# A start-up history load moved from GpSimd's casting queue to SyncE as fp32, with casting loads issued ahead of the identity

## Chip, cores, metric

One core of one Trainium2 chip. The metric is device time in microseconds (us) of that core for one execution.

## The reference

A causal convolution along the sequence with matrix taps: eight shifted copies of `x`, each multiplied by a 512x512 matrix, summed in fp32.

```python
B, S, D, K = 8, 4096, 512, 8          # x: (B, S, D), kernel: (K, D, D), fp32
for k in range(K):
    shifted = x moved k steps down the sequence, zeros in front
    out += np.matmul(shifted, kernel[k])
```

## The kernel before

The sequence is cut into 256-step runs, one run on each of the 128 partitions. The kernel works in bf16 and replaces the eight taps by a three-level scheme of sums and differences: three "nodes" (LO, HI, MID) a step, each of a few 512-wide products. Sums of `x` go to tiles `D4`, `D42`, `D41`, `D421`, `T4`...; differences of weights (`mid_dve`) go to `W[...MID...]`. Only the head of the program is touched by the change. It needs a **history**: the last 7 steps of the run before, which lies one partition lower, so 127 rows are loaded into partitions 1 to 127 (partition 0 and every 16th have no run before them and get zeros).

```python
def load(out, src):                               # casting fp32 -> bf16 load, GpSimd's queue
    nc.gpsimd.dma_start(out=out, in_=src)
...
H = D421                                          # bf16
load(H[1:P, 4:8], xr[0:P - 1, RUN - 4:RUN, :])    # history: 127 rows of 8 KB
load_x(0, 0)
ident = spool.tile([P, P], bf, name="ident")
make_identity(nc, ident)
identh = ...                                      # ident with every 16th column zeroed (GpSimd)
identn = ...                                      # -ident (GpSimd); not used in the head
...
def sums_pe(name, k, *sums):                      # transposes AND adds x and history on TensorE:
    ...                                           # matmul(x, ident) + matmul(H, identh) in one bank
for r in range(2):
    for k in range(4):
        fill(pair(k))                             # 16 dummy matmuls through ident
...
load_w(4)
transpose_pe("xh", 2, H, 5, 8)
sums_pe("d4a", 1, (-4, 0), (-3, 1))
load(H[1:P, 1:4], xr[0:P - 1, RUN - 7:RUN - 4, :])   # second history load, 6 KB rows
load_w(6)
sums_pe("d4b", 2, (-2, 2), (-1, 3))
...                                               # load_w(5), load_w(7)
direct(0, 2)                                      # first products: 16 "direct" ones of 4 matmuls
...
node_a1(1)                                        # first product of the first node
```

`xin` tiles have two buffers, refilled by `load_x` on GpSimd's queue.

```python
mpool = ctx.enter_context(tc.tile_pool(name="m", bufs=2))
...
    elif n.a == MID:
        ms[b_] = mpool.tile([P, 2, D], f32, name="ms")
        nc.scalar.copy(out=ms[b_], in_=p)         # waits for the buffer's earlier store
```

## Time and profile before

| | before |
|---|---|
| time, median of 3 runs | 783.0 us (782.42 to 783.3) |
| span of the profiled run | 780.9 us |
| TensorE | 767.4 us busy, 98% |
| VectorE / ScalarE | 84% / 36% |
| last product ends | 776.35 us |

What a change of the head can win or lose is the time up to 776.35 us in which no product runs: some 24 us in this kernel, 21.2 of them before 28.99 us.

### The profile page before, as it was taken

What the parts mean: (1) busy time and instruction counts of PE and PEld (TensorE: products, weight loads), DVE (VectorE), ACT (ScalarE), POOL (GpSimd) and SP (SyncE); (2) the same over time, 40 slices, a digit from 0 to 9 for tenths busy, and PEclk for the clock granted to TensorE, in tenths of its full rate; (3) what the DMA queues carried; (4) which work ended last, traced back from release to release, by engine and by line L of the source; (5) the groups of instructions that cost most, each with busy time, mean ns of one, the idle gap of its engine ahead of it and who ended that gap; (6) DMA issues with size and microseconds to landing.
All of it is one profiled execution on the core that took longest, in us unless ns stands there. A gap on an engine that the chain in (4) does not pass through costs nothing.

```text
span 780.9 us, 9507 instructions
## 1 busy us (share of the span) xinstructions
PE 767.4 (98%) x3620; PEld 349.0 (45%) x3620; DVE 659.3 (84%) x764; ACT 283.2 (36%) x460; POOL 42.8 (5%) x83
## 2 busy tenths in 40 slices
PE   7899999999999999999999999999999999999997
PEld 4444444444444444444444444444444444444443
DVE  4899888888888889888898888898888898888895
ACT  2453433333333333343324343333343333343332
POOL 5000000000000000000000000000000000000000
PEclk9999999999999999999999999999999999999999
DMA  9963979778788777878777788877787877788753
GB/s 163 210 120 114 237 176 207 169 187 167 178 179 206 174 176 173 177 184 194 184 171 168 179 190 188 191 166 179 165 187 187 195 170 182 166 172 200 179 153 123
DMA packets 159229, 138.37 MB, mean 177 GB/s; under 512 B 130130, under 2 KB 134226, under 8 KB 159184
## 3 DMA queue, kind: packets, MB, share of 16 engines
q1 hardware_dynamic: 145312, 98.84, 46.3%
q0 software_dynamic: 13728, 38.66, 31.1%
q8 instruction: 28, 0.46, 0.2%
q10 hardware_dynamic: 144, 0.26, 0.1%
q14 instruction: 17, 0.14, 0.1%
HBM read 77.32 MB, written 67.11 MB: 185 GB/s over the span
## 4 chain that ended last, share of the span: by engine, by line
PE 94%; DMA 3%; DVE 1%; POOL 1%; issue 0%; ACT 0%; DVEq 0%; POOLq 0%
PE pp L215 94%; DMA xin<-in_x_dram 2%; DMA XT<-xin 1%; POOL w L80 0%; DVE D L76 0%; PE pp L192 0%; DVE pp L76 0%; ACT XT L390 0%; DVE y L76 0%; POOL D L80 0%; DVEq L648 0%; POOL xin L80 0%; POOL identn L148 0%; PE pp L186 0%; POOL ident masks.py:199 0%
## 5 line engine op out<-in xcount | busy, mean ns | idle before, releaser
L215 PE MATMUL pp<-w,D 128*128 128x512 bf16 x3280 | 715.8, 379 | 1.7 <-DMA w<-in_kernel_dram 0.9
L215 PEld LDWEIGHTS <-D 128*128 128x128 bf16 x3280 | 320.2, 98 | 390.4 <-issue 2.8
L76 DVE TENSOR_TENSOR D<-D 128x2048 bf16<-128x2048 bf16 (+2 forms) x250 | 227.2, 948 | 3.4 <-ACT D L369 3.4
L76 DVE TENSOR_TENSOR y<-pp,ms 128x1024 f32<-128x1024 f32 (+1 forms) x121 | 146.4, 1212 | 45.3 <-PE pp L215 45.3
L76 DVE TENSOR_TENSOR D<-XT 128x2048 bf16<-128x2048 bf16 (+2 forms) x153 | 142.5, 947 | 12.1 <-DMA XT<-xin 10.4
L262 ACT COPY pp<-pp 128x512 f32<-128x512 f32 x95 | 54.1, 570 | 260.6 <-PE pp L215 260.6
L274 ACT COPY pp<-pp 128x512 f32<-128x512 f32 x95 | 54.2, 570 | 167.1 <-PE pp L215 165.6
L76 DVE TENSOR_TENSOR pp<-dts,pp 128x512 f32<-128x512 f32 x95 | 65.7, 691 | 43.9 <-ACT dts L280 42.6
L317 ACT COPY ms<-pp 128x1024 f32<-128x1024 f32 x60 | 61.0, 1016 | 35.0 <-PE pp L215 33.0
L80 POOL DMA_DIRECT2D xin<-in_x_dram x64 | 34.0, 531 | 692.5 <-DMA XT<-xin 675.8
L290 DVE SCALAR_TENSOR_TENSOR pp<-pp,dts 128x512 f32<-128x512 f32 x95 | 66.0, 695 | 3.2
L280 ACT COPY dts<-pp 128x512 f32<-128x512 f32 x95 | 57.5, 606 | 0.0
L276 ACT ACTIVATE pp<-pp 128x512 f32<-128x512 f32 x95 | 56.1, 590 | 0.8 <-PE pp L215 0.8
L215 PE MATMUL pp<-w,XT 128*128 128x512 bf16 x120 | 30.8, 379 | 0.0
L76 DVE TENSOR_TENSOR w<-w,w 128x2048 bf16<-128x2048 bf16 x19 | 22.9, 1219 | 1.5 <-DMA w<-in_kernel_dram 1.3
L215 PEld LDWEIGHTS <-XT 128*128 128x128 bf16 x120 | 11.7, 98 | 14.2
L186 PE MATMUL pp<-zero,ident 128*128 128x512 bf16 x20 | 6.7, 493 | 3.1 <-POOL ident masks.py:199 3.1
L215 PE MATMUL pp<-w,F 128*128 128x512 bf16 x36 | 8.7, 379 | 0.2 <-DVE pp L76 0.2
L215 PE MATMUL pp<-w,w 128*128 128x512 bf16 x36 | 8.3, 379 | 0.0
L192 PE MATMUL pp<-ident,xin 128*128 128x128 bf16 x48 | 3.2, 219 | 3.6 <-DMA xin<-in_x_dram 1.4
L80 POOL DMA_DIRECT2D w<-in_kernel_dram x8 | 6.1, 785 | 0.5 <-DMA w<-in_kernel_dram 0.5
L358 DVE COPY D<-pp 128x1536 bf16<-128x1536 bf16 x1 | 1.0, 958 | 6.1 <-PE pp L192 6.1
(59 smaller groups left out, 78.7 us busy)
## 6 DMA issues: line engine op xcount, KB each, us to landing
out_dram<-y SPq DMA_DIRECT2D x123, 512.0 KB, 3.4
xin<-in_x_dram POOLq DMA_DIRECT2D x64, 512.0 KB, 6.0
w<-in_kernel_dram POOLq DMA_DIRECT2D x8, 512.0 KB, 15.7
out_dram<-ms SPq DMA_DIRECT2D x2, 512.0 KB, 5.4
out_dram<-f SPq DMA_DIRECT2D x2, 512.0 KB, 6.3
XT<-xin SPq DMA_TRANSPOSE x61, 6.1
D<-in_x_dram POOLq DMA_DIRECT2D x1, 508.0 KB, 5.6
D<-in_x_dram POOLq DMA_DIRECT2D x1, 381.0 KB, 9.4
```

The lines of the kernel that those rows point to most:

```text
L76: nc.vector.tensor_tensor(out=o, in0=a, in1=b, op=op)
L80: nc.gpsimd.dma_start(out=out, in_=src)
L186: nc.tensor.matmul(pw[:, h], lhsT=ident, rhs=zero, start=True, stop=True)
L192: nc.tensor.transpose(o[:, t - t0, c * P:(c + 1) * P], src[:, t, c * P:(c + 1) * P], ident)
L215: nc.tensor.matmul(bank, lhsT=comp[:, c * P:(c + 1) * P], rhs=w[:, c, :], start=start and c == 0, stop=c == DC - 1, skip_group_check=True)
L262: nc.scalar.copy(out=n.q[:, 0], in_=n.q[:, 1])
L274: nc.scalar.copy(out=n.p[b_][:, 1], in_=n.q[:, 1])
L276: nc.scalar.mul(out=n.p[b_][:, 1], in_=n.q[:, 1], mul=-1.0)
L280: nc.scalar.copy(out=n.dts, in_=n.q[:, 0])
L290: nc.vector.scalar_tensor_tensor(out=p[:, 0], in0=p[:, 1], scalar=-1.0, in1=n.dts, op0=MUL, op1=SUB)
L317: nc.scalar.copy(out=ms[b_], in_=p)
L358: nc.vector.tensor_copy(out=XF[:, 0:3], in_=bank["xh"])
```

## The change

Its intent, as the edit shows it: take the history off GpSimd's queue, so that `x`, weights and the second history load start sooner; load it as plain fp32 from SyncE and cast it on ScalarE and VectorE; issue the first weight and the second history load before building the identity; replace the small matmuls by transposes and VectorE additions; let the dummy matmuls multiply a tile of zeros, so that they needn't wait for the identity; and build one weight difference with ScalarE and an accumulating DMA instead of VectorE.

```diff
-    H = D421
-    load(H[1:P, 4:8], xr[0:P - 1, RUN - 4:RUN, :])
+    H, HF = XT, D421.bitcast(f32).rearrange("p (t b) d -> p t (b d)", b=2)
+    nc.sync.dma_start(out=HF[1:P], in_=xr[0:P - 1, RUN - 4:RUN, :])
     load_x(0, 0)
-    ident = spool.tile([P, P], bf, name="ident")
-    make_identity(nc, ident)
-    identh = ... ; identn = ...
...
+    def mid_neg(u, v):
+        nc.scalar.mul(out=W[MID, u, v], in_=W[LO, u, v], mul=-1.0)
+    def mid_acc(u, v):
+        nc.gpsimd.dma_start(out=W[MID, u, v], in_=W[HI, u, v], accum_op=ADD)
+
+    load_w(4)
+    load(H[1:P, 1:4], xr[0:P - 1, RUN - 7:RUN - 4, :])
+    ident = spool.tile([P, P], bf, name="ident")
+    make_identity(nc, ident)
...
-    for r in range(2):
-        for k in range(4):
-            fill(pair(k))
+    for k in range(6):
+        fill(pair(k % 4))
...
-    sums_pe("d4a", 1, (-4, 0), (-3, 1))
...
+    transpose_pe("x0", 2, xin[0, 0], 0, 2)
+    nc.scalar.copy(out=H[:, 6:8], in_=HF[:, 2:4])
+    nc.vector.tensor_copy(out=H[:, 4:6], in_=HF[:, 0:2])
+    transpose_pe("h0", 0, H, 4, 6)
+    nc.vector.tensor_copy(out=XF[:, 4:6], in_=bank["x0"])
+    nc.vector.tensor_copy(out=XF[:, 0:2], in_=bank["h0"])
+    first_run(XF[:, 0:2])                         # zeroes every 16th column
...
+    tt(D4[:, 0:2], XF[:, 0:2], XF[:, 4:6], ADD)
+    direct(0, 0)                                  # the first product
...
-    mid_dve(0, HI, LO)
+    mid_neg(HI, LO)                               # and mid_acc(HI, LO) later
```

(Cut: the rest of the head, up to the first regular step, is the same calls in another order, with the loads, stores and transposes of blocks 2 and 3 among them; from that step on the programs agree.)

More of the change, by code (lines that the diff above doesn't have):

```diff
@@ L136, in pair @@
         return ppool.tile([P, 2, D], f32, name=f"pp{k}")
-    H = D421
-    load(H[1:P, 4:8], xr[0:P - 1, RUN - 4:RUN, :])
+    H, HF = XT, D421.bitcast(f32).rearrange("p (t b) d -> p t (b d)", b=2)
+    nc.sync.dma_start(out=HF[1:P], in_=xr[0:P - 1, RUN - 4:RUN, :])
     load_x(0, 0)
-    ident = spool.tile([P, P], bf, name="ident")
-    make_identity(nc, ident)
-    identh = spool.tile([P, P], bf, name="identh")
-    nc.gpsimd.tensor_copy(out=identh, in_=ident)
-    nc.gpsimd.memset(identh[:, 0:P:G], 0.0)
-    identn = spool.tile([P, P], bf, name="identn")
-    nc.gpsimd.tensor_scalar_mul(out=identn, in0=ident, scalar1=-1.0)
     zero = spool.tile([P, D], bf, name="zero")
@@ L151 @@
     U1 = zero
-    nc.vector.memset(H[0:1], 0.0)
+    nc.vector.memset(HF[0:1], 0.0)
+    nc.vector.memset(H[0:1, 1:4], 0.0)
     def load_w(tap):
@@ L168, in mid_dve @@
         tt(o, u, v, SUB)
-    bank = {}
-    def mid_pe(h, k, *which):
-        o, u, v = mid(*which)
-        bank[which, h] = pair(k)
-        for c in range(2):
-            pw = bank[which, h][:, c]
-            nc.tensor.matmul(pw, lhsT=ident, rhs=u[:, 2 * h + c], start=True, stop=False)
-            nc.tensor.matmul(pw, lhsT=identn, rhs=v[:, 2 * h + c], start=False, stop=True)
-    def mid_act(h, *which):
-        nc.scalar.copy(out=mid(*which)[0][:, 2 * h:2 * h + 2], in_=bank[which, h])
+    def mid_neg(u, v):
[6 more added lines that the diff above has]
+    make_identity(nc, ident)
+    bank = {}
     def fill(pw):
         for h in range(2):
-            nc.tensor.matmul(pw[:, h], lhsT=ident, rhs=zero, start=True, stop=True)
+            nc.tensor.matmul(pw[:, h], lhsT=zero[:, 0:P], rhs=zero, start=True, stop=True)
     def transpose_pe(name, k, src, t0, t1):
@@ L194, in transpose_pe @@
         bank[name] = o[:, 0:t1 - t0]
-    def sums_pe(name, k, *sums):
-        pw = bank[name] = pair(k)
-        for h, ts_ in enumerate(sums):
-            for c in range(DC):
-                for n, t in enumerate(ts_):
-                    src, idt = (xin[0, 0][:, t], ident) if t >= 0 else (H[:, 8 + t], identh)
-                    nc.tensor.matmul(pw[:, h, c * P:(c + 1) * P], lhsT=src[:, c * P:(c + 1) * P],
-                                     rhs=idt, start=n == 0, stop=n == len(ts_) - 1,
-                                     skip_group_check=True)
-    for r in range(2):
-        for k in range(4):
-            fill(pair(k))
+    for k in range(6):
+        fill(pair(k % 4))
     XF = D42
@@ L346, with first_run @@
     C0, C1 = W[MID, HI, MID], W[MID, LO, MID]
-    load_w(4)
-    transpose_pe("xh", 2, H, 5, 8)
-    sums_pe("d4a", 1, (-4, 0), (-3, 1))
-    load(H[1:P, 1:4], xr[0:P - 1, RUN - 7:RUN - 4, :])
+    def first_run(z):
+        nc.vector.memset(z[:, :, 0:D:G], 0.0)
+    fill(pair(3))
+    transpose_pe("x0", 2, xin[0, 0], 0, 2)
+    nc.scalar.copy(out=H[:, 6:8], in_=HF[:, 2:4])
+    n0.p = {0: pair(0), 1: pair(1)}
+    nc.vector.tensor_copy(out=H[:, 4:6], in_=HF[:, 0:2])
+    transpose_pe("h0", 0, H, 4, 6)
@@ L356 @@
+    nc.vector.tensor_copy(out=XF[:, 4:6], in_=bank["x0"])
+    nc.vector.tensor_copy(out=XF[:, 0:2], in_=bank["h0"])
+    first_run(XF[:, 0:2])
+    transpose_pe("xb", 2, xin[0, 0], 2, 4)
+    transpose_pe("h1", 1, H, 6, 8)
+    nc.scalar.copy(out=XF[:, 2:4], in_=bank["h1"])
+    tt(D4[:, 0:2], XF[:, 0:2], XF[:, 4:6], ADD)
+    direct(0, 0)
+    nc.vector.tensor_copy(out=XF[:, 6:8], in_=bank["xb"])
+    first_run(XF[:, 2:4])
     load_w(6)
-    sums_pe("d4b", 2, (-2, 2), (-1, 3))
-    nc.vector.tensor_copy(out=XF[:, 0:3], in_=bank["xh"])
@@ L359 @@
-    transpose_pe("xf", 2, xin[0, 0], 0, 4)
     load_w(5)
-    nc.vector.tensor_copy(out=D4[:, 0:2], in_=bank["d4a"])
-    nc.scalar.copy(out=D4[:, 2:4], in_=bank["d4b"])
-    n0.p = {0: pair(0), 1: pair(1)}
-    fill(pair(3))
+    transpose_pe("he", 2, H, 1, 4)
+    tt(D4[:, 2:4], XF[:, 2:4], XF[:, 6:8], ADD)
+    direct(0, 3)
     load_w(7)
+    nc.vector.tensor_copy(out=F0, in_=XF[:, 4])
     direct(0, 2)
+    direct(2, 2)
+    tt(E4[:, 1:4], bank["he"], XF[:, 1:4], ADD)
     direct(0, 1)
-    direct(0, 3)
@@ L369 @@
-    nc.scalar.copy(out=XF[:, 3:7], in_=bank["xf"])
-    sums_pe("e4a", 2, (-5, -1), (-6, -2))
-    nc.vector.memset(XF[:, 0:3, 0:D:G], 0.0)
-    tt(D2, XF[:, 0:5], XF[:, 2:7], ADD)
-    direct(2, 3)
-    tt(F21, D2[:, 0:4], D2[:, 1:5], ADD)
-    mid_dve(1, LO, HI)
-    sums_pe("e4b", 2, (-7, -3))
-    direct(1, 2)
-    direct(0, 0)
-    load_x(0, 1)
-    tt(D1, XF[:, 2:4], XF[:, 3:5], ADD)
-    mid_dve(2, LO, HI)
-    nc.scalar.copy(out=E4[:, 3:1:-1], in_=bank["e4a"])
-    mid_dve(2, LO, LO)
-    load_x(1, 0)
@@ L385 @@
-    load_w(0)
-    nc.vector.tensor_copy(out=E4[:, 1], in_=bank["e4b"][:, 0])
-    direct(1, 3)
-    direct(1, 1)
+    first_run(E4[:, 1:4])
+    direct(1, 1)
+    tt(D2, XF[:, 1:6], XF[:, 3:8], ADD)
+    load_x(0, 1)
+    direct(1, 0)
+    tt(D1, XF[:, 3:5], XF[:, 4:6], ADD)
+    mid_dve(1, LO, HI)
+    tt(F21, D2[:, 0:4], D2[:, 1:5], ADD)
+    load_x(1, 0)
+    mid_dve(2, LO, HI)
+    load_w(0)
+    mid_dve(2, LO, LO)
+    mid_dve(1, LO, LO)
+    direct(1, 2)
+    load_w(2)
+    direct(1, 3)
@@ L389 @@
+    direct(2, 3)
+    mid_dve(2, LO, MID)
+    mid_neg(HI, LO)
     transpose_pe("x1", 2, xin[0, 1], 0, 4)
-    nc.scalar.copy(out=XT[:, 4:8], in_=bank["x1"])
-    load_w(2)
-    mid_dve(1, LO, LO)
-    direct(1, 0)
+    nc.vector.tensor_copy(out=XT[:, 4:8], in_=bank["x1"])
+    tt(D4[:, 4:8], XF[:, 4:8], XT[:, 4:8], ADD)
+    tt(D42[:, 3], D4[:, 1], D4[:, 3], ADD)
+    direct(2, 0)
     transpose_pe("x2", 2, xin[1, 0], 0, 4)
-    mid_dve(2, LO, MID)
-    load_w(1)
-    tt(D4[:, 4:8], XF[:, 3:7], XT[:, 4:8], ADD)
@@ L398 @@
-    direct(2, 1)
-    nc.vector.tensor_copy(out=XT[:, 2:4], in_=bank["x2"][:, 2:4])
+    prep_d41(HI)
+    direct(3, 3)
+    nc.scalar.copy(out=XT[:, 2:4], in_=bank["x2"][:, 2:4])
+    nc.scalar.copy(out=XT[:, 0:2], in_=bank["x2"][:, 0:2])
+    direct(3, 2)
     prep_d42(HI)
-    nc.scalar.copy(out=XT[:, 0:2], in_=bank["x2"][:, 0:2])
-    nc.scalar.copy(out=C0[:, 0:2], in_=XT[:, 6:8])
     tt(T4, XT[:, 4:8], XT[:, 0:4], ADD)
     direct(3, 1)
-    prep_d41(HI)
-    tt(T42[:, 0:2], D4[:, 6:8], T4[:, 0:2], ADD)
@@ L407 @@
-    direct(3, 0)
-    nc.scalar.copy(out=C1, in_=XT[:, 0:4])
-    direct(2, 0)
-    nc.scalar.copy(out=F0, in_=XF[:, 3])
-    direct(3, 3)
-    fill(pair(2))
-    tt(D41[:, 1], T4[:, 0], T4[:, 1], ADD)
-    load_w(3)
-    tt(T42[:, 2:4], T4[:, 0:2], T4[:, 2:4], ADD)
-    node_a1(1)
-    direct(2, 2)
-    node_e(nodes[0], 0)
-    tt(D41[:, 0], D4[:, 7], T4[:, 0], ADD)
+    fill(pair(2))
+    nc.scalar.copy(out=C0[:, 0:2], in_=XT[:, 6:8])
+    nc.scalar.copy(out=C1, in_=XT[:, 0:4])
+    direct(3, 0)
@@ L420 @@
+    tt(D41[:, 1], T4[:, 0], T4[:, 1], ADD)
+    node_a1(1)
+    tt(D41[:, 0], D4[:, 7], T4[:, 0], ADD)
+    direct(2, 1)
+    load_w(3)
+    tt(T42[:, 0:2], D4[:, 6:8], T4[:, 0:2], ADD)
     node_a0(nodes[1])
     node_u(nodes[1])
-    direct(3, 2)
+    tt(T42[:, 2:4], T4[:, 0:2], T4[:, 2:4], ADD)
+    tt(D421[:, 0], D42[:, 7], T42[:, 0], ADD)
+    load_w(1)
+    prep_d27()
+    load_x(1, 1)
+    node_e(nodes[0], 0)
     mid_dve(1, HI, HI)
+    mid_dve(2, HI, LO)
     node_seed(nodes[1], 0)
-    prep_d27()
+    load_x(2, 0)
@@ L426 @@
     node_dts(nodes[1])
+    node_v(nodes[1], 0)
+    tt(D421[:, 1:4], T42[:, 0:3], T42[:, 1:4], ADD)
+    node_d(nodes[1], 0)
     node_seed(nodes[1], 1)
-    tt(D42[:, 3], D4[:, 1], D4[:, 3], ADD)
-    node_v(nodes[1], 0)
-    tt(D421[:, 0], D42[:, 7], T42[:, 0], ADD)
-    load_x(1, 1)
+    mid_dve(1, HI, LO)
+    mid_dve(2, HI, HI)
     node_v(nodes[1], 1)
-    tt(D421[:, 1:4], T42[:, 0:3], T42[:, 1:4], ADD)
-    node_a1(2)
-    mid_dve(2, HI, LO)
-    transpose_x(1, 1)
-    mid_dve(1, HI, LO)
@@ L438 @@
-    node_d(nodes[1], 0)
-    node_l(nodes[1], 0, LO)
     mid_dve(2, HI, MID)
-    nc.scalar.copy(out=D4[:, 2:4], in_=T4[:, 2:4])
+    node_l(nodes[1], 0, HI)
+    node_e(nodes[0], 1)
     node_d(nodes[1], 1)
     load_x(2, 1)
-    node_e(nodes[0], 1)
+    mid_acc(HI, LO)
+    node_a1(2)
+    node_l(nodes[1], 0, LO)
+    prep_d421(HI)
+    node_e(nodes[1], 0)
+    nc.scalar.copy(out=D4[:, 2:4], in_=T4[:, 2:4])
+    node_a0(nodes[2])
     node_u(nodes[2])
-    node_l(nodes[1], 0, HI)
-    node_e(nodes[1], 0)
@@ L448 @@
-    node_a0(nodes[2])
+    mid_dve(0, HI, HI)
+    node_l(nodes[1], 1, HI)
+    node_seed(nodes[2], 1)
     node_seed(nodes[2], 0)
-    prep_d421(HI)
-    load_x(2, 0)
-    mid_dve(2, HI, HI)
+    transpose_x(1, 1)
     node_l(nodes[1], 1, LO)
-    node_l(nodes[1], 1, HI)
-    nc.scalar.copy(out=U1, in_=XT[:, 0])
-    node_v(nodes[2], 0)
-    prep_d4(HI)
-    nc.scalar.copy(out=D42[:, 3], in_=T42[:, 3])
-    node_seed(nodes[2], 1)
-    node_v(nodes[2], 1)
-    node_dts(nodes[2])
-    mid_dve(0, HI, HI)
+    node_dts(nodes[2])
@@ L463 @@
+    node_v(nodes[2], 0)
+    nc.scalar.copy(out=D42[:, 3], in_=T42[:, 3])
+    prep_d4(HI)
+    node_d(nodes[2], 0)
+    prep_d41(HI)
+    node_v(nodes[2], 1)
+    node_a1(3)
+    node_l(nodes[2], 0, HI)
+    nc.scalar.copy(out=U1, in_=XT[:, 0])
+    node_a0(nodes[3])
     node_e(nodes[1], 1)
-    prep_d41(HI)
-    node_d(nodes[2], 0)
-    node_l(nodes[2], 0, HI)
-    tt(A1[:, 0], C0[:, 1], C1[:, 0], ADD)
+    node_l(nodes[2], 0, LO)
+    node_e(nodes[2], 0)
+    mid_dve(0, LO, LO)
+    node_u(nodes[3])
@@ L468 @@
     prep_d42(HI)
     node_d(nodes[2], 1)
-    transpose_x(2, 0)
+    node_l(nodes[2], 1, HI)
+    node_seed(nodes[3], 0)
+    node_seed(nodes[3], 1)
+    tt(D421[:, 0:4], D42[:, 3:7], D42[:, 4:8], ADD)
     mid_dve(0, LO, HI)
-    node_a1(3)
-    node_l(nodes[2], 0, LO)
-    node_a0(nodes[3])
-    node_e(nodes[2], 0)
-    mid_dve(0, LO, LO)
-    tt(D421[:, 0:4], D42[:, 3:7], D42[:, 4:8], ADD)
-    node_u(nodes[3])
-    node_l(nodes[2], 1, HI)
-    node_seed(nodes[3], 1)
-    node_seed(nodes[3], 0)
+    node_v(nodes[3], 0)
@@ L482 @@
+    node_v(nodes[3], 1)
+    node_l(nodes[2], 1, LO)
+    tt(A1[:, 0], C0[:, 1], C1[:, 0], ADD)
     node_dts(nodes[3])
     mid_dve(1, MID, HI)
-    node_v(nodes[3], 1)
+    node_e(nodes[2], 1)
     node_d(nodes[3], 1)
-    mid_dve(0, HI, LO)
-    node_v(nodes[3], 0)
     node_d(nodes[3], 0)
-    node_l(nodes[2], 1, LO)
     node_a1(4)
     mid_dve(1, MID, LO)
-    tt(D21[:, 2:4], C1[:, 0:2], C1[:, 2:4], ADD)
     node_l(nodes[3], 1, HI)
     node_l(nodes[3], 0, LO)
+    node_a0(nodes[4])
+    node_l(nodes[3], 0, HI)
@@ L495 @@
+    tt(D21[:, 2:4], C1[:, 0:2], C1[:, 2:4], ADD)
     mid_dve(2, MID, MID)
-    node_e(nodes[2], 1)
-    load_x(3, 0)
-    node_l(nodes[3], 0, HI)
-    node_a0(nodes[4])
-    tt(D21[:, 0:2], C0[:, 0:2], C1[:, 0:2], ADD)
-    node_u(nodes[4])
-    node_e(nodes[3], 0)
-    node_l(nodes[3], 1, LO)
-    tt(A1[:, 1], C1[:, 0], C1[:, 1], ADD)
-    mid_dve(2, MID, LO)
+    node_dts(nodes[4])
+    tt(D21[:, 0:2], C0[:, 0:2], C1[:, 0:2], ADD)
+    node_e(nodes[3], 0)
+    node_u(nodes[4])
+    node_seed(nodes[4], 0)
@@ L506 @@
+    tt(A1[:, 1], C1[:, 0], C1[:, 1], ADD)
+    node_l(nodes[3], 1, LO)
+    mid_dve(2, MID, LO)
+    node_seed(nodes[4], 1)
+    load_x(3, 0)
+    node_v(nodes[4], 0)
+    node_a1(5)
     mid_dve(2, MID, HI)
-    node_seed(nodes[4], 0)
-    node_v(nodes[4], 0)
-    node_seed(nodes[4], 1)
-    node_dts(nodes[4])
+    node_e(nodes[3], 1)
+    transpose_x(2, 0)
     node_d(nodes[4], 0)
-    node_a1(5)
     node_v(nodes[4], 1)
@@ L515 @@
     node_l(nodes[4], 0, HI)
+    node_d(nodes[4], 1)
     node_l(nodes[4], 0, LO)
+    node_u(nodes[5])
     node_a0(nodes[5])
-    node_e(nodes[3], 1)
-    node_d(nodes[4], 1)
-    node_u(nodes[5])
     node_seed(nodes[5], 0)
     node_l(nodes[4], 1, LO)
-    tt(F21[:, 0], D2[:, 0], D21[:, 0], ADD)
-    node_l(nodes[4], 1, HI)
     node_y(nodes[4], 0, LO)
     node_y(nodes[4], 0, HI)
+    tt(F21[:, 1], D21[:, 0], D21[:, 1], ADD)
+    prep_d4(LO)
+    node_l(nodes[4], 1, HI)
+    node_dts(nodes[5])
@@ L527 @@
+    tt(F21[:, 0], D2[:, 0], D21[:, 0], ADD)
+    node_v(nodes[5], 0)
+    node_y(nodes[4], 1, LO)
     store(0, LO, 0, first[0, LO, 0])
-    tt(F21[:, 1], D21[:, 0], D21[:, 1], ADD)
-    node_dts(nodes[5])
-    node_v(nodes[5], 0)
+    store(0, HI, 0, first[0, HI, 0])
+    node_d(nodes[5], 0)
+    node_seed(nodes[5], 1)
     prep_d27()
-    node_seed(nodes[5], 1)
-    store(0, HI, 0, first[0, HI, 0])
+    node_v(nodes[5], 1)
+    node_a1(6)
+    node_l(nodes[5], 0, LO)
+    node_a0(nodes[6])
     load_x(3, 1)
-    node_y(nodes[4], 1, LO)
@@ L536 @@
-    node_v(nodes[5], 1)
-    node_d(nodes[5], 0)
+    node_y(nodes[4], 1, HI)
+    transpose_x(2, 1)
     node_d(nodes[5], 1)
+    node_l(nodes[5], 0, HI)
+    store(0, HI, 1, first[0, HI, 1])
     tt(F21[:, 2:4], D21[:, 1:3], D21[:, 2:4], ADD)
-    node_l(nodes[5], 0, LO)
-    node_l(nodes[5], 0, HI)
-    node_a1(6)
+    prep_d41(LO)
+    node_y(nodes[5], 0, HI)
+    node_u(nodes[6])
+    node_y(nodes[5], 0, LO)
     node_l(nodes[5], 1, HI)
-    node_u(nodes[6])
-    prep_d4(LO)
     store(0, LO, 1, first[0, LO, 1])
-    node_y(nodes[4], 1, HI)
@@ L548 @@
-    node_a0(nodes[6])
-    node_y(nodes[5], 0, LO)
-    prep_d41(LO)
-    transpose_x(2, 1)
-    node_l(nodes[5], 1, LO)
-    store(0, HI, 1, first[0, HI, 1])
     node_seed(nodes[6], 0)
     node_v(nodes[6], 0)
-    node_y(nodes[5], 0, HI)
+    node_dts(nodes[6])
+    store(1, LO, 0, first[1, LO, 0])
+    node_seed(nodes[6], 1)
     tt(D21[:, 0:2], D2[:, 0:2], D2[:, 1:3], ADD)
-    node_dts(nodes[6])
-    node_seed(nodes[6], 1)
+    node_l(nodes[5], 1, LO)
+    prep_d42(LO)
+    store(1, HI, 0, first[1, HI, 0])
@@ L560 @@
+    node_d(nodes[6], 0)
+    node_y(nodes[5], 1, HI)
     node_v(nodes[6], 1)
+    node_y(nodes[5], 1, LO)
     tt(D21[:, 2:4], D2[:, 2:4], D2[:, 3:5], ADD)
-    node_d(nodes[6], 0)
-    prep_d42(LO)
-    node_y(nodes[5], 1, HI)
+    store(1, HI, 1, first[1, HI, 1])
+    node_a1(7)
     node_d(nodes[6], 1)
-    store(1, LO, 0, first[1, LO, 0])
-    node_y(nodes[5], 1, LO)
-    store(1, HI, 0, first[1, HI, 0])
-    node_a1(7)
-    store(1, HI, 1, first[1, HI, 1])
     prep_d4(HI)
```

## The prediction

> **What bounds the kernel now.** I read, in this order, the page's busy times, the chain that ended last in order of time, TensorE's timeline of the first 50 us, the windows table for what the DMA engines move, and the DMA issues. The page and the chain:
>
> ```profile
> PE 767.4 (98%) x3620; PEld 349.0 (45%) x3620; DVE 659.3 (84%) x764; ACT 283.2 (36%) x460; POOL 42.8 (5%) x83
> ...
> 7.61 17.42 DMA xin<-in_x_dram
> ...
> 48.79 21.96 PE pp L215 x100
> ...
> 97.28 679.08 PE pp L215 x3144
> 776.35 0.02 issue
> ```
>
> TensorE sets the time. From 97.28 us on, 3144 products follow one another without a hole: 679.08/3144 = 0.216 us each. The program has 3280+120+36+36 = 3472 such products (the page's L215 rows), so 3472 x 0.216 = 750.0 us that no reordering removes. The tail from 776.35 to 780.9 is 4.6 us. The other 780.9 - 750.0 - 4.6 = 26.3 us are all that a change of the head can win. They lie here:
>
> ```profile
> 3.10 5.51 PE L186 MATMUL pp<-zero,ident 128*128 128x512 bf16 x16 [3.10 <-POOL ident masks.py:199]
> ...
> 13.81 2.75 PE L215 MATMUL pp<-w,D 128*128 128x512 bf16 x12
> 17.29 1.03 PE L215 MATMUL pp<-w,D 128*128 128x512 bf16 x4
> 20.07 3.61 PE L215 MATMUL pp<-w,D 128*128 128x512 bf16 x16 [0.91 <-DMA w<-in_kernel_dram]
> 25.08 1.07 PE L192 MATMUL pp<-ident,xin 128*128 128x128 bf16 x16 [1.40 <-DMA xin<-in_x_dram]
> 25.98 1.03 PE L215 MATMUL pp<-w,w 128*128 128x512 bf16 x4
> 28.10 1.05 PE L192 MATMUL pp<-ident,xin 128*128 128x128 bf16 x16 [1.09 <-ACT XT L390]
> 28.99 3.62 PE L215 MATMUL pp<-w,w 128*128 128x512 bf16 x16
> ```
>
> At 28.99 us, 12+4+16+4 = 36 products are done (7.8 us of work): 21.2 us lost. The remaining 5.1 us go in small waits up to 97 us. The head is a race with the loads. How fast these are:
>
> ```profile
> 0.00:1.00 1.00, 0.00 (x0) 0.00 (x0) 0.15 (x1) 0.28 (x1) 0.19 (x4) 1.00 0.00 0
> ...
> 5.00:6.00 1.00, 1.00 (x3) 0.30 (x2) 0.00 (x0) 0.00 (x0) 1.00 (x2) 1.00 1.04 209
> ...
> 73.00:74.00 1.00, 1.00 (x7) 0.44 (x5) 1.00 (x3) 0.00 (x0) 0.00 (x0) 1.00 1.02 418
> ```
>
> The last two columns are the DMA engines' busy share and GB/s as written. From 5 to 6 us casting loads run at 209 GB/s of bf16, that is 418 GB/s of fp32 read. From 73 to 74 us, where plain fp32 stores run from SyncE's queue, it is 418 too. So 16 engines move 418 GB/s either way: **26.1 GB/s for one engine**. And the issues, with KB and median us to landing:
>
> ```profile
> out_dram<-y SPq DMA_DIRECT2D x123, 512.0 KB, 3.4
> ...
> D<-in_x_dram POOLq DMA_DIRECT2D x1, 508.0 KB, 5.6
> ```
>
> A store of 0.524 MB needs 1.25 us at 418 GB/s and lands after 3.4: some 2.1 us is fixed. The old history load (127 rows of 8 KB, cast, from GpSimd) lands after 5.6 us, so it must have run on many engines: on one, its 1.04 MB would take 40 us.
>
> **What the Trainium skill says.** "DMA: Bandwidth & Descriptors", section "Why a DMA increments its semaphore by 16 and not by 1", tells how many engines a DMA uses: the largest count up to 16 that divides the size of the slowest dimension of both sides. It names 127 partitions as a case for one engine, and an exception for GpSimd's direct copies, which put 127 partitions on all 16. The 5.6 us above agree with the exception; the trace before has no 127-row DMA from SyncE, all of its DMAs have 128 rows, so the rule itself is untested here. The same page, "Queues, rings and completion order", says that each engine goes round-robin over the queues that have work; not seen either, as only GpSimd's queue is busy in the head. "TensorE: Matmul & The Clock Gate", section "What's actually happening", has the clock halved after about 3.4 us of idling until it was busy as long. The trace agrees: the first fills load weights every 0.43 us, later products follow at 0.216.
>
> **The change part by part.**
>
> 1. History. It moves from GpSimd's casting load to SyncE as fp32, still 127 rows. In the built program it is one DMA of 127 rows of 2048 elements on either side, not split. By the rule it goes to one engine: 127 x 8192 B = 1.040 MB / 26.1 GB/s = 39.8 us by itself. That engine also carries a sixteenth of the casting loads queued from the start: each 1 MB load gives it 65 KB. If descriptors alternate one for one (8 KB of history against 8 KB of x, 2 KB of weights or 6 KB of the second history load), then during x (8 descriptors), the first weight (32), the second history (8), two weights (64) the history gets 112 of its 127 rows, and the last 15 pass during the fourth weight. The engine has then moved 1.04 + 0.34 MB: 53 us. Issue near 0.9 + fixed 2.1 + 53 = **56 us landing** (call it T0).
> 2. What hangs on it. VectorE's queue has the history's cast ahead of the copies of x's transposes; TensorE's has the history's transposes ahead of all 64 first products. The first product waits for T0, not for 13.81 us. GpSimd's queue stops too: the second x block needs the first one's buffer, freed by transposes behind the history; four weights stand behind it. They need some 2.5 us each once released, and are wanted 20 us later: hidden.
> 3. Removed on TensorE: 56 small matmuls (sums through the identities) and 4 fills; added 16 history transposes. At about 0.055 us this is 2 us, in a time when TensorE waits anyway. The identity's two derived copies (0.29+0.13+0.54 us on GpSimd) go, and the first weight is issued about 1.5 us sooner: nothing, with T0 where it is.
> 4. After T0, by durations of the rows before: history cast 1.1 us (VectorE), 8 transposes at half clock 1.1, copies 0.7+0.7, add 0.7: first product at about T0+4; the next needs the second half's copies, T0+6.6. Then 36 products (7.8) reach the transposes of block x1 at T0+14.4. But VectorE has in its one queue, from T0+6: F0, E4, D2, D1, F21 and five weight differences of 1.22 us (11.5 us in all), then x1's copy (1.3) to T0+19, and D4, D42, D41, T4 (5.1) to T0+24. The first node's product waits for that last sum: T0+24 with 60 products (13.0) done, so **11 us lost beyond T0**. Before, these sums ran beside the loads; now they start after them.
> 5. Node 1 then waits 1.4 us for its difference behind two more weight differences; the small waits up to 97 us were 5.1 and I keep 3.6, since the loads are no longer scarce then. The middle weight by ScalarE (one pass, 1.9 us by its 2048-wide copies) and an accumulating DMA takes 1.2 us from VectorE and is wanted late: nothing on the path.
>
> Sum: T0 56 + 11 + 1.4 + 3.6 + 750.0 + 4.6 = 826.6 for the span; the run before is 783.0 for a span of 780.9, so + 2.1: **828.7 us**.
>
> **The rivals.**
> (a) SyncE's load is spread over 16 engines after all. Against it: the rule and the unsplit shape. For it: GpSimd's exception, and the change only makes sense to someone who counts on it. Then the same 8.1 MB must land before block x1 as before, beginning perhaps 0.7 us sooner; 40 instead of 32 products are done by then (1.7 us). 783.0 - 0.7 - 1.7 = about **780**, within 2%.
> (b) One engine, but the history has it to itself (served first): 0.9 + 2.1 + 39.8 = 43 us, so **816**. Strictly the other way, history last behind all seven queued casts (0.44 MB): 60 us, **832**.
> (c) VectorE's backlog after T0 is smaller or larger than the 11 us: if fp32 casts or the half clock cost more, +3; if the copies hide, -4. It moves the result, not its sign.
>
> **Range and chances.** One engine has about 0.86 for me, and all its variants lie in 812 to 840. The spread variant has 0.13, near 780. The range of 8 in 10 is 806 to 842. Faster by over 2% (below 767.3) would take 16 of the 26 us of loss away: 0.01. Within 2%: 0.13. Slower: 0.86.
>
> **What would show it.** The history DMA's landing between 43 and 60 us, by far the longest to landing; a GB/s of about 26 in the windows of the head once the other loads have stopped; an idle time of TensorE of some 45 us put down to the history (or to the ScalarE and VectorE casts behind it); the first product near 60 us, then weights never waited for; the long stretch of products at 0.216 us unchanged. It is wrong if the history lands before 12 us; then the time is 780 and TensorE's first waits are for x or weights as before. It is wrong in size if T0 is right but TensorE is dense earlier or later than T0+24.

## The result

| | before | after |
|---|---|---|
| median of 6 runs | 783.28 us (782.42 to 783.77) | 828.87 us (827.96 to 834.02) |
| span of the profiled run | 780.9 us | 826.4 us |
| mean granted clock | 0.998 | 0.966 |

The ratio is 1.0592, with a 95% interval of 1.0565 to 1.0619. Here and below a ratio is the mean time of one kernel's fast runs over that of the other's of the same rounds, so not quite the ratio of the medians quoted.

The busy-time line of the page of the changed kernel, and its chain that ended last (start, length, what):

```profile
PE 766.5 (93%) x3576; PEld 348.4 (42%) x3576; DVE 661.5 (80%) x771; ACT 281.7 (34%) x459; POOL 42.3 (5%) x80
```

```profile
4.07 52.84 another core or an unknown queue
...
94.75 183.55 PE pp L198 x848
...
279.28 542.58 PE pp L198 x2512
821.86 0.02 issue
```

TensorE has the same work to do: 0.9 us less busy time, and 44 fewer instructions (56 small matmuls and 4 fills gone, 16 transposes come). Its products still take 542.58/2512 = 0.216 us. What is new is 52.84 us near the start, on something that the chain can't name: SyncE's load. The timeline of the changed kernel (start, length, engine, line, operation; in brackets the engine's idle time before it and what ended it) names it:

```profile
0.74 0.35 SPq L141 DMA_DIRECT2D D<-in_x_dram  x1
...
11.92 1.03 PE L187 MATMUL pp<-ident,xin 128*128 128x128 bf16 x8 [5.70 <-DMA xin<-in_x_dram]
...
57.01 0.69 DVE L343 CAST XT<-D 128x1024 bf16<-128x1024 f32 x1 [52.94 <-DMA D<-in_x_dram]
57.76 1.03 PE L187 MATMUL pp<-ident,XT 128*128 128x128 bf16 x8 [44.81 <-DVE XT L343]
...
60.70 1.89 PE L198 MATMUL pp<-w,D 128*128 128x512 bf16 x4 [0.20 <-DVE D L76]
...
75.06 1.05 PE L187 MATMUL pp<-ident,xin 128*128 128x128 bf16 x16 [2.03 <-DVE XT L386]
...
79.99 1.04 PE L198 MATMUL pp<-w,D 128*128 128x512 bf16 x4
```

The history is issued at 0.74 us and lands 56 us later. VectorE sat idle 52.94 us for it, TensorE 44.81 us behind VectorE's cast. The first product starts at 60.70 us instead of 13.81. The windows table of the changed kernel (window, its length, busy us and count of TensorE, weight loads, VectorE, ScalarE, GpSimd; then TensorE's clock, the DMA engines' busy share, GB/s):

```profile
18.00:20.00 2.00, 0.00 (x0) 0.00 (x0) 0.00 (x0) 0.00 (x0) 0.00 (x0) 0.50 1.16 233
20.00:25.00 5.00, 0.00 (x0) 0.00 (x0) 0.00 (x0) 0.00 (x0) 0.00 (x0) 0.50 0.23 54
30.00:35.00 5.00, 0.00 (x0) 0.00 (x0) 0.00 (x0) 0.00 (x0) 0.00 (x0) 0.50 0.07 24
...
50.00:55.00 5.00, 0.00 (x0) 0.00 (x0) 0.00 (x0) 0.00 (x0) 0.00 (x0) 0.50 0.06 22
```

and one row of the same table of the kernel before:

```profile
20.00:25.00 5.00, 3.61 (x16) 1.46 (x15) 3.64 (x4) 0.00 (x0) 0.00 (x0) 1.00 1.14 219
```

From some 25 to 57 us the DMA engines together move 22 to 24 GB/s (bytes as written, so a casting load counts half of what it reads) at a busy share of 0.06 to 0.07: one engine of sixteen (1/16 = 0.0625). Nothing else moves.

The trace's own records of the semaphores say it most directly. Each of these transfers raises its semaphore by 16, a casting load in single updates as engines finish. A SyncE load can show one early update and then fewer single ones; the size of the early one isn't recorded and is taken as what is missing to 16. Times of the 15th and the 16th update, in us:

| load | before: 15th / 16th | after: 15th / 16th |
|---|---|---|
| history | 6.8 / 6.9 (cast) | +15 at once at 1.2, then 56.9 |
| x, block 0 | 9.3 / 9.4 | 6.5 / 11.9 |
| weight, tap 4 | 12.3 / 12.5 | 9.4 / 25.8 |
| second history | 14.2 / 14.3 | 11.3 / 30.6 |
| weight, tap 6 | 16.8 / 16.8 | 14.1 / 43.5 |
| weight, tap 5 | 19.3 / 20.0 | 16.5 / 56.6 |
| weight, tap 7 | 21.9 / 22.6 | 19.0 / 59.4 |
| x, block 1 | 24.3 / 25.0 | 21.4 / 61.8 |

Fifteen engines are done with every load after the history 2.7 to 2.9 us **sooner** than before: that is the intent, and it worked. The sixteenth holds the history and delivers its share of every other load late. So the change costs twice over: the history is late, and so is everything queued next to it.

### The profile page after: what moved, and what is told of

Read it like the earlier page. It is cut to its first block, busy times and chain, and to the rows that moved or that the text cites. A ratio compares the mean times of both kernels' runs of the same rounds, so it can differ in the third digit from the quotient of the medians.

```text
span 826.4 us, 9431 instructions
## 1 busy us (share of the span) xinstructions
PE 766.5 (93%) x3576; PEld 348.4 (42%) x3576; DVE 661.5 (80%) x771; ACT 281.7 (34%) x459; POOL 42.3 (5%) x80
## 4 chain that ended last, share of the span: by engine, by line
PE 89%; another core or an unknown queue 6%; DVE 3%; issue 1%; ACT 0%; DVEq 0%; ACTq 0%
PE pp L198 89%; DVE w L76 1%; DVE D L76 1%; PE pp L187 0%; DVE D L146 0%; DVE pp L76 0%; ACT pp L257 0%; DVE XT L386 0%; DVE F L76 0%; DVE XT L343 0%; DVE D L346 0%; DVE XT L147 0%; DVE y L76 0%; DVE pp L273 0%
## 5 line engine op out<-in xcount | busy, mean ns | idle before, releaser
L76 DVE TENSOR_TENSOR D<-D 128x1024 bf16<-128x1024 bf16 (+1 forms) x252 | 228.3, 945 | 0.2 <-issue 0.2
L187 PE MATMUL pp<-ident,XT 128*128 128x128 bf16 x28 | 3.2, 290 | 44.8 <-DVE XT L343 44.8
L187 PEld LDWEIGHTS <-XT 128*128 128x128 bf16 x28 | 2.7, 136 | 45.6 <-DVE XT L343 45.1
L76 DVE TENSOR_TENSOR w<-w,w 128x2048 bf16<-128x2048 bf16 x18 | 21.4, 1215 | 0.1
L198 PEld LDWEIGHTS <-XT 128*128 128x128 bf16 x120 | 11.7, 98 | 14.2
```

Source lines behind the costliest of these rows:

```text
L76: nc.vector.tensor_tensor(out=o, in0=a, in1=b, op=op)
L187: nc.tensor.transpose(o[:, t - t0, c * P:(c + 1) * P], src[:, t, c * P:(c + 1) * P], ident)
L198: nc.tensor.matmul(bank, lhsT=comp[:, c * P:(c + 1) * P], rhs=w[:, c, :], start=start and c == 0, stop=c == DC - 1, skip_group_check=True)
```

## Experiments

Twelve kernels were run, in three calls; each call's kernels share one chip and the runs of the kernel before. Medians of the kernel before: 783.55 us (first call, 11 runs), 783.35 (second, 9), 783.8 (third, 9). All kernels were correct but one.

### First call: is it the row count?

**a_split112.** The changed kernel with the load cut in two, 112 + 15 rows; same bytes, queue and type.

```diff
-    nc.sync.dma_start(out=HF[1:P], in_=xr[0:P - 1, RUN - 4:RUN, :])
+    nc.sync.dma_start(out=HF[1:113], in_=xr[0:112, RUN - 4:RUN, :])
+    nc.sync.dma_start(out=HF[113:P], in_=xr[112:P - 1, RUN - 4:RUN, :])
```

> The changed kernel with its history load cut in two, 112 rows and 15 rows, same bytes, same queue, same fp32. Theory (the engine count is the largest divisor of the row count up to 16; 127 gives one, 112 gives 16, 15 gives 15): history landed by about 9 us, first product near 13 us, 780 us in all (775 to 785). Rival 1 (SyncE's fp32 load is slow for its size, its queue or its shifted rows, not for the number 127): landing stays near 57 us and the time near 829. Rival 2 (the change is slow for its order on VectorE and TensorE too, only partly for the landing): the landing goes to 9 us, but the time stays over 790.

Measured: 785.75 us median, just above the expected range, ratio 1.001 (0.9984 to 1.0036). The 112 rows gave 16 single updates, the last at 6.7 us; the 15 rows gave one at once and 15 that came by 7.2. The 45 us are gone, with fp32, SyncE, the casts and all the reordering still there. Its TensorE timeline:

```profile
12.66 0.82 PE L199 MATMUL pp<-w,D 128*128 128x512 bf16 x3 [0.31 <-DVE D L76]
...
24.46 1.07 PE L188 MATMUL pp<-ident,xin 128*128 128x128 bf16 x16 [1.64 <-DMA xin<-in_x_dram]
...
27.82 1.03 PE L199 MATMUL pp<-w,D 128*128 128x512 bf16 x4
```

Before 27.82 us 44 products are done (9.5 us), so 18.3 us are lost, 2.9 less than the 21.2 before. Yet the time isn't better. The six runs are 785.67, 785.87, 785.84, 780.91, 780.18 and 787.52: two of them are some 3 us below the kernel before, as the head's gain would have it, and the other four are 5 to 7 us above these two. The profiled run (785.67), one of the four, shows where the time goes, in its timeline at 77 to 97 us:

```profile
76.83 0.53 POOL L80 DMA_DIRECT2D xin<-in_x_dram  x1 [18.04 <-DMA XT<-xin]
77.04 0.33 SPq L284 DMA_DIRECT2D out_dram<-ms  x1
...
85.63 1.01 ACT L301 COPY ms<-pp 128x1024 f32<-128x1024 f32 x1 [5.40 <-DMA out_dram<-ms]
...
87.18 10.01 PE L199 MATMUL pp<-w,D 128*128 128x512 bf16 x37 [3.28 <-ACT pp L258]
```

An `x` load and the store of `ms` are issued within 0.2 us of each other. The store takes 8.6 us to let the buffer go (77.04 to 85.63), ScalarE waits 5.40 us for it, TensorE 3.28 us behind ScalarE. This is a second theory, tested below.

**b_split122.** The same with 122 + 5 rows. 122 is 2 x 61, so the rule predicts two engines.

> Cut into 122 and 5 rows; 122 = 2 x 61. Theory: two engines with 61 rows each (5 rows on five engines): 0.5 MB each, sharing one for one with the casting loads, about 0.71 MB until done, 27 us: landing near 30 us, time about 802 (797 to 808), and in the landings of each casting load two engines late instead of one. Rival (either all engines or one): 780 or 825.

Measured: 807.37 us, ratio 1.0304. The 122 rows gave +14 at once at 1.2 us, then single updates at 30.9 and 32.1. VectorE's cast in its timeline, and a row of its windows:

```profile
32.59 0.69 DVE L344 CAST XT<-D 128x1024 bf16<-128x1024 f32 x1 [28.52 <-DMA D<-in_x_dram]
```

```profile
25.00:30.00 5.00, 0.00 (x0) 0.00 (x0) 0.00 (x0) 0.00 (x0) 0.00 (x0) 0.50 0.13 44
```

Two engines move 44 GB/s, twice the 22 of the 127-row load. The cast comes 24.4 us sooner than in the changed kernel and the median is 21.5 us lower. Part of the difference is the same `ms` wait: here TensorE waits 3.8 us for ScalarE at 110 us.

**d_split113.** 113 + 14 rows; 113 is prime, so one engine again, though the transfer is cut in two.

> The same cut one row further on: 113 rows and 14 rows. 113 is prime. Theory: the 113 rows go to one engine again, 0.93 MB instead of 1.04: landing about 4 to 5 us sooner than 56.9 (the engine still shares with the casting loads), so 51 to 54 us, time about 824 (820 to 828). Rival (it is the one large DMA, or 127 itself, that was slow): as the cut at 112, near 780.

Measured: 825.01 us (822.87 and 827.15), ratio 1.0529; the 113 rows came +15 at once, then one update at 51.4 us. So it isn't the cutting that helps in a_split112, it is the divisor. One thing is unexplained here, in the timeline of d_split113:

```profile
1.16 19.81 SPq L142 DMA_DIRECT2D D<-in_x_dram  x1
```

SyncE's queue was held 19.81 us in issuing the second, 14-row load. It didn't matter (the first load is later), and it didn't happen behind the 122-row load, nor in g_bystander, where a 127-row load stands behind another one and both are issued in 0.89 us. The profiled run (827.15) also has the `ms` wait, 2.10 us of TensorE at 128.6 us.

**e_pool_history.** History as GpSimd's casting load again, all the rest of the change kept.

```diff
-    nc.sync.dma_start(out=HF[1:P], in_=xr[0:P - 1, RUN - 4:RUN, :])
+    load(H[1:P, 4:8], xr[0:P - 1, RUN - 4:RUN, :])
-    nc.scalar.copy(out=H[:, 6:8], in_=HF[:, 2:4])
-    nc.vector.tensor_copy(out=H[:, 4:6], in_=HF[:, 0:2])
```

> The changed kernel without its history part: the history is loaded by GpSimd with a cast straight into the tile, first in GpSimd's queue as before (127 rows, no casts after it); everything else of the change stays. Theory (the history part alone makes the change slow): landing about 7 us as in the kernel before, time 778 to 783. Rival 2 (order and middle weight cost too): over 786.

Measured: 784.35 us median (782.09 to 786.85), above the expected 778 to 783, ratio 1.0007 (0.9988 to 1.0025). Everything in the change but the history's queue costs nothing that can be measured. Its runs too fall into two groups, near 782.5 (three) and near 786 (three), and its profiled run (786.13) shows a 2.62 us wait of TensorE for ScalarE at 86.9 us, the place of the `ms` wait.

### Second call: the wait for the `ms` store, and the small parts

**k_split_gate.** a_split112, with both loads of block 3 held by a one-column GpSimd copy that waits for a sum, so that no `x` load should meet the `ms` store.

```diff
-    load_x(3, 0)                       # and load_x(3, 1), from their places
+    nc.gpsimd.tensor_copy(out=gate[:, 0:1], in_=D41[:, 0, 0:1])
+    load_x(3, 0)
+    load_x(3, 1)
```

> The 112 and 15 cut, and the x load that was issued at 76.8 us held on GpSimd until a sum of VectorE near 82 us is done (a one-column copy on GpSimd reads it). In the cut kernel ScalarE waited 5.4 us for the store of an ms tile (issued 77.0, landed 85.5) and TensorE 3.3 us behind it, and its runs fell into two groups, near 780.5 and 786. Theory (the store shares the DMA engines with that x load): the store lands near 81 to 82, the wait goes, all runs near 780 (779.5 to 781.5). Rival (the store waits behind the stores ahead of it on SyncE's queue alone): the wait and the two groups stay.

Measured: 787.16 us, ratio 1.0052 (1.0039 to 1.0064). **A miss**, and the timeline says why:

```profile
75.90 0.55 POOL L80 DMA_DIRECT2D xin<-in_x_dram  x1 [0.33 <-issue]
...
77.28 0.53 POOL L80 DMA_DIRECT2D xin<-in_x_dram  x1 [0.84 <-DMA XT<-xin]
77.60 0.33 SPq L285 DMA_DIRECT2D out_dram<-ms  x1
...
87.71 1.01 ACT L302 COPY ms<-pp 128x1024 f32<-128x1024 f32 x1 [6.92 <-DMA out_dram<-ms]
```

The first of the two loads had been issued near 58 us in a_split112; my gate moved it to 75.90. Now two loads stand beside the store instead of one. The store took 10.1 us instead of 8.6, ScalarE waited 6.92 us instead of 5.40, TensorE 4.80 instead of 3.28. The gate was wrong, but the dose speaks for the theory.

**i_gate_dvemid** (k_split_gate with the weight difference on VectorE again) and **j_gate_ident_first** (k_split_gate with the identity built before the loads).

```diff
-    mid_neg(HI, LO)
-    mid_acc(HI, LO)
+    mid_dve(0, HI, LO)
```

> The same, with the middle weight made by VectorE again (one subtraction of 1.2 us where the kernel before has it) instead of ScalarE's negated copy and the accumulating DMA. Theory (off the path): within 1.5 us of the held version, either sign. Rival (the part is worth something, as VectorE is busy 9 to 10 tenths in the head): 1.2 us or more slower.

```diff
+    ident = spool.tile([P, P], bf, name="ident")
+    make_identity(nc, ident)
     load_w(4)
     load(H[1:P, 1:4], xr[0:P - 1, RUN - 7:RUN - 4, :])
-    ident = spool.tile([P, P], bf, name="ident")
-    make_identity(nc, ident)
```

> The same as the held version, with the identity made on GpSimd ahead of the first weight load and the second history load, as in the kernel before. Theory: the identity's two instructions and their issue take 0.6 us of GpSimd, so these loads start 0.6 us later; but the engines are still busy with the history and the first x block then, so the loads' landings move by 0 to 0.6 us: 0 to 0.6 us slower.

Measured: 788.0 us (786.47 to 788.26) and 786.82 us (786.38 to 788.09), against 787.16 (786.84 to 788.24) for k_split_gate in the same rounds. Both differences lie inside the scatter: neither part of the change is worth anything measurable. A caution: all three carry the `ms` wait, which could hide a gain that comes before it.

**m_narrow_mids.** The changed kernel with five weight differences of VectorE cut from 2048 to 64 columns (the rest zeroed; wrong, relative error 0.84), to test how much of the loss after the landing is VectorE's backlog.

```diff
+    def mid_narrow(*which):
+        o, u, v = mid(*which)
+        tt(o[:, 0, 0:64], u[:, 0, 0:64], v[:, 0, 0:64], SUB)
...
-    mid_dve(1, LO, HI)                 # and four others
+    mid_narrow(1, LO, HI)
```

> A wrong result on purpose: the changed kernel as it is (127 rows, one engine), but the five weight differences that VectorE makes between the history and block x1's copy are cut to 64 columns each (the rest of these weights is set to 0 by GpSimd while it idles). History landing stays near 57. My step 4 said that VectorE's backlog after the landing, 5 x 1.22 us of it these differences, delays the first node's product to about 24 us after the landing (measured 23.1). Theory (backlog): VectorE copies x1 as soon as it is transposed, 1.5 to 2 us earlier, and the first node's product starts 1.5 us or more earlier after the landing; the rest of the 6 us is lost to TensorE's own work. Rival (TensorE's chain alone sets it): no change there.

Measured: 829.8 us, ratio 1.0593. History landed at 56.4; the first node's product began at 77.93 us, 21.5 after it, against 23.1 in the changed kernel. So of that stretch only 1.6 us are those five differences (five at 1.22 us). Here VectorE waits 3.42 us for TensorE's transposes of block 1 before it copies them, so the rest is not VectorE's backlog. The 1.6 us don't show in the time: this run has the `ms` wait (TensorE loses 2.6 us by it) and the profiled run of the changed kernel has not. Its timeline:

```profile
130.47 1.01 ACT L304 COPY ms<-pp 128x1024 f32<-128x1024 f32 x1 [4.68 <-DMA out_dram<-ms]
```

### Third call: a better gate, and the one engine by itself

**k2_split_gate2.** a_split112 with only the second load of block 3 held, by a sum that is done near 82 us.

```diff
-    load_x(3, 1)
...
     tt(D21[:, 2:4], D2[:, 2:4], D2[:, 3:5], ADD)
+    nc.gpsimd.tensor_copy(out=gate[:, 0:1], in_=D21[:, 3, 0:1])
+    load_x(3, 1)
```

> The 112 and 15 cut with the right x load held. My first hold was a miss: it moved the x block that had been issued at 58 us to 75.9, so that two x blocks ran beside the ms store, and the store's landing went from 8.5 us after its issue to 10.1, ScalarE's wait from 5.4 to 6.9, all runs to 787. Now the earlier block stays and the one issued at 76.8 waits for a VectorE sum that ends at 82.1. Theory (the store shares the engines with x loads): the store lands near 81.5, ScalarE waits under 2 us, TensorE not, all runs near 780.3 (779.5 to 781.5). Rival (the store waits for SyncE's own queue): the two groups 780.5 and 786 stay.

Measured: 781.96 us median (782.13, 782.04, 781.96, 780.66, 781.83), 0.5 us above the expected range, ratio 0.9974 (0.9961 to 0.9986). Timeline:

```profile
77.06 0.33 SPq L285 DMA_DIRECT2D out_dram<-ms  x1
...
81.35 1.01 ACT L302 COPY ms<-pp 128x1024 f32<-128x1024 f32 x1 [1.10 <-PE pp L200]
...
82.81 0.53 POOL L80 DMA_DIRECT2D xin<-in_x_dram  x1 [0.32 <-issue]
```

With the `x` load at 82.81 the store lands 4.2 us after its issue (its 16th update is at 81.25) and is out of the way by 81.35: ScalarE waits for TensorE now, not for a DMA. The 5-us group of runs is gone. This is the fastest kernel, 0.26% ahead of the kernel before. In most runs it stays about 1.4 us above the two good runs of a_split112 (on another chip); its profile has a 1.33 us wait of TensorE for VectorE at 96.5 us that I didn't trace further.

**e2_pool_gate2.** e_pool_history with the same gate.

> The same hold in the version whose history comes by GpSimd's casting load: no wait for the ms store either, and so what the history's own place is worth when it is spread: the cut SyncE load against GpSimd's. Theory: the casting load keeps GpSimd's queue 0.68 us longer before the other loads and x1 lands 0.8 us later in the traces (24.4 against 25.3 for TensorE's transposes), so 0.8 us slower than the held cut version: 781.1 (780.3 to 782.3).

Measured: 782.07 us (781.71 to 783.39), ratio 0.9977 (0.9963 to 0.999). Once the history is spread over the engines, SyncE with fp32 and GpSimd with a cast are the same within 0.3 us, far inside the interval; the 0.8 us that I expected between them don't show.

**f_alone.** The changed kernel with all GpSimd loads held until the history has landed: what the one engine takes by itself.

```diff
     nc.sync.dma_start(out=HF[1:P], in_=xr[0:P - 1, RUN - 4:RUN, :])
+    nc.gpsimd.tensor_copy(out=gate[:, 0:1], in_=HF[:, 0, 0:1])
     load_x(0, 0)
```

> The changed kernel (127 rows on SyncE), with all of GpSimd's loads held behind the history by a one-column copy that reads it. Theory (one engine at 26.1 GB/s; the 14 us on top in the changed kernel are the casting loads' share of that engine): the history lands at 0.9 + 2.1 + 39.8 = 42.8 us instead of 56.9; the head then starts 42 us late: time 780.3 + 42 = 822 (820 to 829 with the store's wait). Rival (57 us is what such a DMA takes by itself, at 18 GB/s): it still lands near 57, time near 836.

Measured: landing at 42.3 us, 824.6 us (824.5 and 824.7), ratio 1.0521. A row of its windows:

```profile
15.00:20.00 5.00, 0.00 (x0) 0.00 (x0) 0.00 (x0) 0.00 (x0) 0.00 (x0) 0.50 0.06 26
```

1.040 MB at this 26 GB/s are 40 us, and the other 2.3 us are the issue and the fixed part (an estimate from this row). Sharing the engine with the casting loads therefore delays the history by 56.9 - 42.3 = 14.6 us. But taking the sharing away wins only 4 us of the median. The loads then start at 43 us, and block 1 of x lands at 64.1, even later than in the changed kernel (61.8). The first node's product comes 8.5 us earlier (71.45 us), but 2.8 us of that go again in the `ms` wait, which this run has at 125.9 us and the profiled run of the changed kernel has not; the rest I didn't trace.

**g_bystander.** The kernel **before**, its casting history untouched, with the same bytes and 127 rows loaded a second time from SyncE into tiles that nothing reads.

```diff
+    for j in range(2):
+        nc.sync.dma_start(out=fpool.tile([P, 2, D], f32, name="f")[1:P],
+                          in_=xr[0:P - 1, RUN - 4 + 2 * j:RUN - 2 + 2 * j, :])
     load(H[1:P, 4:8], xr[0:P - 1, RUN - 4:RUN, :])
```

> The kernel before, with the same bytes (127 rows, 8 KB each, as two DMAs of 4 KB rows) loaded from SyncE's queue at the start into two tiles that nobody reads until 55 us or later; nothing waits for them in the head. Theory (the one engine delays its sixteenth of every casting load behind the rows it carries, and a load is landed only when all 16 are): each casting load has one engine late as in the changed kernel; block x1 lands near 60 instead of 25 and the time is about 783 + 35 = 818 (812 to 826). Rival (only the wait for the history costs): 783, at most 2 us more.

Measured: 825.03 us (824.86 and 825.2), ratio 1.0527: 41 us more, for transfers that nobody waits for (they landed at 37.9 and 72.7 us; the tiles are first written by ScalarE at 102.3 us, and that waited for TensorE). TensorE's timeline:

```profile
34.25 1.87 PE L219 MATMUL pp<-w,D 128*128 128x512 bf16 x4 [6.90 <-DMA w<-in_kernel_dram]
...
54.10 1.89 PE L196 MATMUL pp<-ident,xin 128*128 128x128 bf16 x16 [6.84 <-DMA xin<-in_x_dram]
```

The kernel's own loads are late: the 16th update of x's block 1 came at 54.1 us instead of 25.0, its 15th at 24.3. So the second half of the damage is real by itself: one busy engine of sixteen holds up every transfer that has a share on it.

## Why the prediction was right

The products are counted as 3484, 752.5 us.

| step of the prediction | predicted | measured |
|---|---|---|
| landing of the history | 56 us | 56.9 |
| first product after it | +4 | +3.8 (60.70) |
| first node's product after it | +24 | +23.1 (79.99) |
| lost beyond the landing | 11 | 10.1 (23.1 less 60 products, 13.0) |
| later waits | 5.0 | 2.4 (821.86 - 752.5 - 56.9 - 10.1) |
| products | 750.0 (3472) | 752.5 (3484), 0.216 us each, unchanged |
| tail | 4.6 | 4.5 |
| time outside the span | 2.1 | 1.8 |
| time | 828.7 | 828.87 median |

1. **One engine.** Shown in four ways: one late update of 16; 22 to 24 GB/s at a busy share of 0.06; twice that with 122 rows; and no loss with 112 + 15. Rival (a), the spread load, fell.
2. **Sharing by alternation.** Right, and the trace's records of single DMA packets, which no view prints, show it: between 30.6 and 43.5 us one 8192-byte row of history (0.32 us) and one 1024-byte row of weight (0.10 us; 2 KB as read) follow each other without exception. Rival (b), the engine to itself or the history last, fell: alone it lands at 42.3 us. A size was off: 20 rows of history had started when x's last share landed at 11.9 us, where I had 8. With the next four loads (16th updates at 25.8, 30.6, 43.5 and 56.6 us) another 32, 9, 33 and 33 went, so the history ended with the third weight, not 15 rows into the fourth. That the landing still came out within 1 us is partly luck. The engine worked from 1.73 to 56.55 us, 54.8 us where I had 53: it moved less, 1.35 MB as read, but at 24.7 GB/s on average, not 26.1. And the issue and the fixed part took 2.1 us where I had 3.0.
3. **What hangs on the landing.** The order of cast, transposes, copies and sum was right. VectorE's cast took 0.69 us, not the 1.1 I took from a row of the profile before. The loss beyond the landing, rival (c), was 10.1 us instead of 11. But step 4 and (c) put it down to VectorE's queue, and that is right only in small part. A row of the windows, from the first transpose of history to the first node's product:

```profile
57.76:79.99 22.23, 20.00 (x131) 11.38 (x131) 19.82 (x26) 8.22 (x8) 4.61 (x7) 0.88 0.97 159
```

TensorE was busy 20.0 of these 22.2 us, 13.0 of them being what 60 products take at full clock. So some 7 us of the 10.1 are its own transposes, dummy matmuls and first matmuls at half clock; 2.2 us are idle, nearly all of it the 2.03 us that it waits for VectorE's copy of block 1 at 75.06 us; and 0.9 us pass before its first transpose. VectorE's last sum ends at 79.93 us, as TensorE comes to need it. m_narrow_mids agrees: without the five differences it gains 1.6 us.
4. **Hidden parts.** Weights are never waited for after the landing, as predicted: TensorE has no wait for a DMA between 57.76 and 94.75 us. Node 1's wait of 1.4 us for its weight difference isn't seen as such: there are 0.66 us for ScalarE at 84.27 and 0.66 for VectorE at 94.75. The later waits come to 2.4 us and not 5.0, as the 5.1 us of small waits read from the kernel before held the 12 products left out (2.6 us). Both kernels run these, so the sum was not hurt. The middle weight, the identity's place and the smaller transposes are worth nothing measurable (i, j, e). The halved clock during the wait is in the windows (0.50).
5. **What I missed.** Rival (a) was put at 780. The head did gain what that asked for (2.9 us in a_split112, 2.4 predicted), but in most runs an `x` load and the `ms` store meet later on, and TensorE waits some 3 us: 785.75 median. That this meeting is the cause is shown by taking it away (k2_split_gate2: store free by 81.35 us, no wait; e2_pool_gate2 likewise for TensorE) and by making it worse (k_split_gate). It isn't the earlier head that brings the two together, since kernels with a late head have the wait too (b_split122, d_split113, f_alone, m_narrow_mids). In the changed order of calls the transpose that frees the `x` buffer runs 5.2 us before the `ms` store (71.85 and 77.04 us in a_split112), in the kernel before 3.0 us (74.96 and 77.96). I had not looked at what the new order would make coincide. The changed kernel has the meeting as well, in its timeline, and yet no wait of TensorE for it:

```profile
124.54 0.53 POOL L80 DMA_DIRECT2D xin<-in_x_dram  x1 [22.11 <-DMA XT<-xin]
124.60 0.33 SPq L283 DMA_DIRECT2D out_dram<-ms  x1
...
128.90 1.01 ACT L300 COPY ms<-pp 128x1024 f32<-128x1024 f32 x1 [1.11 <-PE pp L198]
```

Here the load is issued 0.06 us before the store, and the store landed after 4.2 us. In the six profiles where one load is issued 0.2 to 0.4 us before it (a, b, d, e_pool_history, f, m) the store took 7.3 to 9.0 us, and in the four where the load comes 1.8 us or more behind it (the kernel before, g, k2, e2) 3.7 to 4.6. So tenths of a microsecond seem to decide, which would make the two groups of runs; this isn't shown, as no fast run of a_split112 has a profile. The changed kernel's one run of 834.02 us lies about 5 us above the others, which is the size of the wait's group; that run has no profile either, so this stays open. Open too is why SyncE held one issue for 19.8 us in d_split113.

## What to carry to other kernels

In all seven row counts tried here, a plain load issued from SyncE was as wide as the largest number up to 16 that divides its row count: cut 127 rows into 112 + 15, or keep such a load on GpSimd with its cast, and check by counting the single semaphore updates of each SyncE transfer. One overloaded DMA engine delays not only its own transfer but every other transfer with a share on it, so a narrow load costs even where nobody waits for it. And when calls are put in another order, look at which later load and store this makes coincide, before crediting the gain.

## What the Trainium skill lacked or had wrong

- "DMA: Bandwidth & Descriptors", section "Why a DMA increments its semaphore by 16 and not by 1": its rule for the number of engines held in every case seen on SyncE (rows -> single late updates: 127 -> 1, 113 -> 1, 122 -> 2, 5 -> 5, 14 -> 14, 15 -> 15, 112 -> 16), and so did its exception for GpSimd (127 rows landed at 6.9 us). It doesn't say what this costs others: the 16th update of x's block 1 went from 25.0 to 61.8 us, and two unread 127-row loads cost 41 us (g_bystander).
- Same page, "Issuing engines are not separate DMA queues": it says that issuing from several engines only saves the sequencer's time. Here the choice of queue, with the cast that went with it, also set the number of DMA engines, and cost 45 us; queue and cast were not told apart. (e2_pool_gate2 against k2_split_gate2 agrees with the page once both are spread: 782.07 and 781.96 us.)
- Same page, "Rules for kernel authors": the row on using all 16 engines warns of an outermost dimension below 16 and asks for a multiple of 16. It doesn't say that 127 and 113 rows, well above 16, get one engine (the section named first has 127); nor that cutting such a load, 112 + 15 rows, is a cure (785.75 against 828.87 us).
- Same page, "Queues, rings and completion order": round-robin between queues agrees. It gives packets of some 9 to 17 descriptors as the unit; here the engine changed queues after every single row (8192 bytes of history, 1024 of weight; 33 and 32 of them between 30.6 and 43.5 us).
- No page that I read explains why SyncE was held 19.8 us in issuing a second load behind a 113-row one, and not behind a 122-row one or, in g_bystander, a 127-row one.
